# Second product of the stick-breaking scores over 128 rows, with the queries' low parts stored twice

## The chip, the cores and the metric

The kernel runs on one NeuronCore of one Trainium2 chip. The metric is device time in microseconds (us): the median of the runs of one program. The engines are named as the profile names them: PE is TensorE's matmul, PEld its weight load, DVE VectorE, ACT ScalarE, POOL GpSimd, SP the queue that issues most DMAs.

## The reference, cut to what matters

A decoder trunk of two layers over 512 tokens of width 1024, in float32. Each layer projects the normed input into three branches (latent attention, stick-breaking attention, retention), merges them by gates and adds an MLP. The change is in the second branch, whose queries, keys and values have 8 heads of 64:

```
z = einsum('bqhd,bkhd->bhqk', q[:, start:end], k[:, :end]) * scale
before = s_idx < t_idx
log_not = where(before, log_sigmoid(-z), 0.0)
between = cumsum(log_not, axis=3, reverse=True) - log_not
a = where(before, exp(log_sigmoid(z) + between), 0.0)
out = einsum('bhqk,bkhd->bqhd', a, v[:, :end])
```

`start` and `end` bound a block of 128 queries, so the blocks see 128, 256, 384 and 512 keys.

## The kernel before

**Precision.** TensorE reads float32r, which holds fewer bits than float32. Every operand of a product is therefore split into a high part (ScalarE's copy into float32r) and a low part (VectorE's difference), and a product is made of several: a dense tile of 128 columns by 512 tokens (`mm_T`, L456) is 8 times three products, high by high (L462), high by low (L463), low by high (L464), all with 128 rows of contraction and 512 columns, added up in one PSUM bank. `mm_N` (L466) does the same with 256 columns (L474 to L476). The weights stream from DRAM in chunks of up to 1 MB and are split in units (L104), up to four units at a time in the buffers `whi` and `wlo`.

**Stick-breaking operands.** Heads go in pairs. `put_q` (L909) reads a dense tile's bank with the queries of one pair, head 0 in partitions 0 to 63 and head 1 in 64 to 127, scales it to `f`, and writes three tiles: `a` with head 0's high part in both halves, `b` with head 1's high part in both halves, and `lo` with the two low parts, each in its own half. `put_k` (L924) writes for head 0 [high | low] and for head 1 [low | high]. All are tiles of a ring of 44 slots of 128 by 512 (named `slot`); a tile given back goes to the ring's end.

**The scores.** `stick_breaking`'s `first` (L585) makes one unit: pair p, query tile i, both heads. For a head the first product (L592) takes the high queries, stored twice, against [high | low] keys: 128 rows of contraction give high by high and high by low at once. The second (L593) takes the low queries, 64 rows, against the 64 rows of the high keys. Both add into one half of a two-bank PSUM tile `z`. The number of columns is 128 (i + 1), but at least 256. Then VectorE masks (L541), ScalarE takes the sigmoids, VectorE the running product (L604) and the product of both (L605). Two units later TensorE transposes the result (L548), and after a pair's fourth unit multiplies it with V (L556, in halves of 64 columns).

**Order.** The units are put between the steps of dense tiles by the driver: `advance` (L278) lets a unit through when a count of dense work has come far enough, so 16 units of a layer are spread over about 120 us of dense products. In this stage the dense products have two banks, `d`, in turn. A scheduler of the framework then orders the instructions of each engine. Pairs 0 and 1 get their queries and keys before the units start, pairs 2 and 3 while they run. Retention's scores (L691) are products of 64 rows too, on the two halves in turn; they are not touched.

Of the kernel before, what the change touches and what calls it, by code (L numbers as in the profile page):

```python
# [28 lines left out]
GATE_RUN = (2, 2, 4)  # tiles of gates before their branch products  # L29
SC = 96.0**-0.5  # L30

# columns of w_in
# [3 lines left out]
# columns of the constant pack  # L36
# [8 lines left out]
# rows of the gain pack  # L45
# [3 lines left out]
class Weights:  # L49
    """Streams weight chunks from DRAM and splits each unit into two float32r parts."""  # L50
# [16 lines left out]
    def chunk(self, srcs, k, cols, units):  # L67
        """srcs: list of (dram view [p, k, c], column); units: list of (k0, k1, c0, c1, form)"""
        c = len(self.chunks)
        self.chunks.append((srcs, k, cols))  # L70
        self.left.append(len(units))
        for u in units:
            self.units.append((c, u))
# [18 lines left out]
    def split(self):  # L92
        nc = self.nc
        u = self.n_split
        c, (k0, k1, c0, c1, form) = self.units[u]
        s = self.free.popleft()
        self.slot[u] = s
        self.n_split += 1
        src = self.raw(c)[:, k0:k1, c0:c1]
        nk, w = k1 - k0, c1 - c0  # L100
        if form is None:
            hi = self.his[s][:, : nk * w].rearrange("p (k c) -> p k c", c=w)
            lo = self.los[s][:, : nk * w].rearrange("p (k c) -> p k c", c=w)
            self.last = (nc.scalar.copy(hi, src).ins, nc.vector.tensor_sub(lo, src, hi.bitcast(F32)).ins)  # L104
        elif form == "kv":
            # [head, key | value, 64] to [key | value, head, 64]
            hi = self.his[s][:, : nk * w].rearrange("p (k c) -> p k c", c=w)
            lo = self.los[s][:, : nk * w].rearrange("p (k c) -> p k c", c=w)
            for k in range(nk):
                a = src[:, k].rearrange("p (h s d) -> p h s d", s=2, d=64)  # L110
                b = hi[:, k].rearrange("p (s h d) -> p h s d", s=2, d=64)
                nc.scalar.copy(b, a)
                nc.vector.tensor_sub(lo[:, k].rearrange("p (s h d) -> p h s d", s=2, d=64), a, b.bitcast(F32))
        else:
            # a head's 96 columns of w_uq, as [64 | 32 | 32 swapped] or [32 | 32 swapped | 64]
            w = 128
            hi = self.his[s][:, : nk * w].rearrange("p (k c) -> p k c", c=w)
            lo = self.los[s][:, : nk * w].rearrange("p (k c) -> p k c", c=w)
            if form == 0:
                parts = [(0, 0, 96), (96, 80, 16), (112, 64, 16)]  # L120
            else:
                parts = [(64, 0, 64), (0, 64, 32), (32, 80, 16), (48, 64, 16)]
            for dst, at, n in parts:
                nc.scalar.copy(hi[:, :, dst : dst + n], src[:, :, at : at + n])
            for dst, at, n in parts:
                nc.vector.tensor_sub(
                    lo[:, :, dst : dst + n], src[:, :, at : at + n], hi[:, :, dst : dst + n].bitcast(F32)
                )
        self.views = getattr(self, "views", {})
        self.views[u] = (hi, lo)  # L130
        self.left[c] -= 1
        if self.left[c] == 0:
            self.dma()
# [20 lines left out]
def trunk_kernel(  # L154
# [23 lines left out]
    # ---------------------------------------------------------------- buffers  # L178
# [36 lines left out]
    # the functions of one table set are issued together  # L215
# [11 lines left out]
    def table(out, in_, func, **kw):  # L227
        """an activation from the table set in use"""
        i = nc.scalar.activation(out, in_, func, **kw).ins
        tc.add_manual_dep(i, phase["first"].name, order, reason="table set")  # L230
        phase["all"].append(i)

    # ---------------------------------------------------------------- driver
# [24 lines left out]
    def lend():  # L258
        """between attentions their banks serve the dense products"""
        dt.extend(spare)  # L260
# [8 lines left out]
    def evacuate(ps, fn):  # L269
        """run fn a little later; then ps may be written again"""  # L270

        def go():
            fn()
            waiting[id(ps)] = False

        defer(go)
# [38 lines left out]
    # ---------------------------------------------------------------- weights  # L315
# [3 lines left out]
    def plan_T(ap, width=256):  # L319
        """columns for transposed outputs, in units of 128"""  # L320
        v = planes(ap, 0)
        nk, cols = v.shape[1], v.shape[2]
        for c in range(0, cols, width):
            w = min(width, cols - c)
            step = 1024 // nk
            W.chunk([(v[:, :, c : c + w], 0)], nk, w, [(0, nk, a, a + min(step, w - a), None) for a in range(0, w, step)])
# [53 lines left out]
    # ---------------------------------------------------------------- constants  # L380
# [30 lines left out]
    # per-token statistics -----------------------------------------------------  # L411
    def to_rstd(ms, n, width, power=-0.5):
        """(ms / n + EPS) ** -0.5 for a [128, width] sum of squares"""
        a = tiny()
        nc.vector.tensor_scalar(a[:, :width], ms, 1.0 / n, EPS, op0=ALU.mult, op1=ALU.add)
        r = tiny()
        nc.gpsimd.tensor_tensor(r[:, :width], a[:, :width], mhalf[:, :width], op=ALU.pow)
        return r

    def token_sums(parts, n=NT):  # L420
        """sums over the partitions of all parts [128, 128 n] as [128 tokens, n]"""
# [8 lines left out]
    def row_sums(ps, sq):  # L430
        """sums over the partitions of sq, on every partition"""
        nc.tensor.matmul(ps, ones.to_broadcast([P, P]), sq, start=True, stop=True)

    def spread_to(ps, r, n=NT):
        """ps[:, token] = r[token] on every partition"""
# [10 lines left out]
    def split_to(hi, lo, src, g=None):  # L446
        """hi + lo = src * g"""
# [7 lines left out]
    # products -----------------------------------------------------------------  # L455
    def mm_T(ps, wh, wl, xs):  # L456
        """ps [128 columns, 512 tokens]; wh, wl: per k [128, 128]; xs: per k (hi, lo)"""
# [9 lines left out]
    def mm_N(ps, wh, wl, xs, t):  # L467
        """ps [128 tokens, N]; wh, wl: per k [128, N]"""
# [13 lines left out]
    class Later:  # L482
        """parts that a deferred step still has to emit"""
# [12 lines left out]
    def tile_T(xs, evac):  # L496
        """the next unit of 128 columns"""
# [7 lines left out]
    def tiles_N(n_units, evac):  # L505
        """the next units, stacked along k, for every token tile"""
# [10 lines left out]
    # ---------------------------------------------------------------- attention  # L517
    flatA = aT.rearrange("p r c -> p (r c)")

    def put_A(i, e, ps):  # L520
        """store the transposed blocks j = 0..i of query tile i and parity e"""
# [16 lines left out]
    def mask(z, i, m):  # L538
        """mask the diagonal blocks of query tile i"""
# [44 lines left out]
    def stick_breaking(qT, kT, v, yb):  # L584
        def first(p, i):  # L585
# [4 lines left out]
            for e in range(2):  # L590
                r = slice(e * 64, (e + 1) * 64)
                nc.tensor.matmul(z[:, e, :M], qT[p][e][:, tok], kT[p][e][:, :M], start=True, stop=False)  # L592
                nc.tensor.matmul(z[:, e, :M], qT[p][2][r, tok], kT[p][e][r, :M], start=False, stop=True)  # L593
            mask(z, i, strict)
            # a[t] = sigmoid(z[t]) * product over t' > t of sigmoid(-z[t'])
# [58 lines left out]
    def retention(l, rq, rk, rv, rg, yc):  # L654
# [28 lines left out]
        def scores(t):  # L683
            # within the chunk, [key, query]
# [19 lines left out]
        def outputs(t):  # L704
            c = st[t]
            y = c["y"] = rot(zt)[:, 0]
            for p in range(PAIRS):
                b = slice(p * P, (p + 1) * P)
                if t:
                    # the state is zero between a pair's heads  # L710
# [9 lines left out]
            if t < NT - 1:  # L720
                # state after the chunk
# [25 lines left out]
        def norms(t):  # L747
            # group norm and gate, natural layout
# [15 lines left out]
            # 2 * silu  # L764
# [42 lines left out]
    # ---------------------------------------------------------------- set-up  # L807
    def setup():
# [35 lines left out]
        def tables():  # L844
            """cos and sin of positions * frequencies"""
# [30 lines left out]
            # per token: cos cos | -sin sin, over sqrt(96)  # L876
# [8 lines left out]
    # ---------------------------------------------------------------- a layer  # L885
    def layer(l, box):
        """box['next']: per-token rstd [128, 4] of the layer's input, once known"""
# [18 lines left out]
        # ---- stick-breaking inputs  # L906
        sq, sk, sv, yb = {}, {}, [get() for _ in range(NT)], {}

        def put_q(p):  # L909
            # per head [hi | hi], and the lo parts of the pair  # L910
            def go(ps):
                f, a, b, lo = get(), get(R), get(R), get(R)
                nc.vector.scalar_tensor_tensor(f, in0=ps, scalar=0.125, in1=rstd_b, op0=ALU.mult, op1=ALU.mult)
                for t, r in ((a, slice(0, 64)), (b, slice(64, 128))):
                    nc.scalar.copy(t[r], f[r])
                    nc.vector.tensor_sub(lo[r], f[r], t[r].bitcast(F32))
                nc.scalar.copy(a[64:128], f[0:64])
                nc.scalar.copy(b[0:64], f[64:128])
                put(f)
                sq[p] = (a, b, lo)  # L920
# [3 lines left out]
        def put_k(p):  # L924
            # per head [hi | lo] or [lo | hi]
# [68 lines left out]
        # ---- latent vectors  # L994
# [26 lines left out]
        def stat_c(key, n):  # L1021
            # the latents still lack their token's rstd, which this folds in
# [39 lines left out]
        # ---- latent attention inputs  # L1062
# [67 lines left out]
        # ---- gates and branches  # L1130
# [58 lines left out]
        # ---- retention inputs, rotated  # L1189
# [45 lines left out]
        # ---- output projection, residual  # L1235
        stats = {}

        def new_x(m, g):
            """xm[m] is final: square it, split it"""
# [26 lines left out]
        # ---- MLP  # L1266
# [92 lines left out]
    # ---------------------------------------------------------------- run  # L1359
# [10 lines left out]
def _constants():  # L1370
    """tables that depend on shapes alone"""
# [29 lines left out]
def _layout(inputs):  # L1401
    """the program's inputs, in its order: x by columns, the gains and positions by partitions"""
# [29 lines left out]
```

## Time and profile before

| What | us |
|---|---|
| median of 3 runs | 1877.92 (1877.71 to 1878.12) |
| span of the profiled execution | 1875.9 |
| PE busy in it | 1857.7 |
| PEld busy | 1533.4 |
| DVE busy | 1064.1 |
| ACT busy | 717.4 |

The span runs from the first to the last instruction of one profiled execution. Products are pipelined, so an engine that is busy for 99% of the span may still be at less than its rate: the distance between the starts of two products tells more than how long one of them is.

### The profile page before, as it was taken

How to read it: one execution, taken by the hardware profiler on the slowest of the kernel's cores; microseconds unless marked ns; L12 is line 12 of the kernel's file. 1: busy time of each engine (PE TensorE's matmuls, PEld its weight loads, DVE VectorE, ACT ScalarE, POOL GpSimd, SP SyncE). 2: the span in 40 equal slices, each digit the busy share in tenths (PEclk: the TensorE clock that was granted, in tenths of full speed). 3: DMA queues.
4: the chain of work that ended last, by engine and by line, in shares of the span. 5: the costliest groups of instructions: out<-in, count | busy, mean ns of one | idle time of the engine just before them, and what ended most of it. 6: DMA issues, size and time to landing. Idle time of an engine off the chain costs nothing.

```text
span 1875.9 us, 23563 instructions
## 1 busy us (share of the span) xinstructions
PE 1857.7 (99%) x9668; PEld 1533.4 (82%) x9668; DVE 1064.1 (57%) x1706; ACT 717.4 (38%) x1191; POOL 42.5 (2%) x57
## 2 busy tenths in 40 slices
PE   8999999999999999999999999999999999999998
PEld 7878877988888888888897787779888888888887
DVE  6775566577555444444638647646764654444456
ACT  5555444233243222323436454432333432323244
POOL 1000000001000000000000000000010000000000
PEclk9999999999999999999999999999999999999999
DMA  5220132122432322332423112221224233223324
GB/s 182 83 86 25 48 100 79 57 69 89 132 104 93 107 93 90 96 105 92 129 76 102 46 36 80 68 88 59 79 90 135 90 99 104 90 90 103 100 92 133
DMA packets 163980, 169.81 MB, mean 91 GB/s; under 512 B 5920, under 2 KB 160048, under 8 KB 163872
## 3 DMA queue, kind: packets, MB, share of 16 engines
q1 hardware_dynamic: 161360, 160.97, 27.4%
q0 software_dynamic: 2368, 7.30, 1.2%
q8 instruction: 76, 1.25, 0.3%
q14 instruction: 32, 0.26, 0.0%
q10 hardware_dynamic: 144, 0.03, 0.0%
HBM read 164.09 MB, written 4.19 MB: 90 GB/s over the span
## 4 chain that ended last, share of the span: by engine, by line
PE 98%; DMA 1%; DVE 1%; issue 0%; ACT 0%; POOLq 0%; SPq 0%; DVEq 0%
PE d L462 24%; PE d L464 24%; PE d L463 24%; PE d L474 4%; PE d L475 4%; PE d L476 4%; PE t L556 3%; PE t L548 2%; PE z L627 2%; PE z L593 1%; PE z L592 1%; DMA raw<-in_w_in_dram 1%; PE z L715 1%; PE z L476 1%; PE z L475 1%; PE z L474 1%
## 5 line engine op out<-in xcount | busy, mean ns | idle before, releaser
L104 ACT CAST whi<-raw 128x1024 fp32r<-128x1024 f32 (+1 forms) x292 | 305.9, 1049 | 672.5 <-PE d L463 552.9
L104 DVE TENSOR_TENSOR wlo<-raw,whi 128x1024 fp32r<-128x1024 f32 (+1 forms) x292 | 354.9, 1216 | 222.2 <-ACT whi L104 221.2
L462 PE MATMUL d<-xh,whi 128*128 128x512 f32 x1072 | 425.5, 397 | 7.0 <-ACT whi L104 7.0
L464 PE MATMUL d<-xh,wlo 128*128 128x512 f32 x1072 | 420.7, 393 | 0.6 <-DVE wlo L104 0.5
L463 PE MATMUL d<-xl,whi 128*128 128x512 f32 x1072 | 421.1, 393 | 0.1
L462 PE MATMUL d<-slot,whi 128*128 128x512 f32 (+1 forms) x960 | 368.5, 384 | 0.3 <-DVE slot L1309 0.3
L464 PE MATMUL d<-slot,wlo 128*128 128x512 f32 (+1 forms) x960 | 362.6, 379 | 0.0
L463 PE MATMUL d<-slot,whi 128*128 128x512 f32 (+1 forms) x960 | 362.1, 379 | 0.0
L462 PEld LDWEIGHTS d<-xh,whi 128*128 128x128 f32 x1072 | 201.9, 188 | 51.8 <-ACT whi L104 7.5
L464 PEld LDWEIGHTS d<-xh,wlo 128*128 128x128 f32 x1072 | 201.8, 188 | 44.5 <-DVE wlo L104 1.7
L463 PEld LDWEIGHTS d<-xl,whi 128*128 128x128 f32 x1072 | 202.0, 188 | 43.1 <-issue 2.4
L462 PEld LDWEIGHTS d<-slot,whi 128*128 128x128 f32 x960 | 180.3, 188 | 37.3 <-DVE slot L1309 0.5
L463 PEld LDWEIGHTS d<-slot,whi 128*128 128x128 f32 x960 | 180.3, 188 | 36.7 <-issue 0.5
L464 PEld LDWEIGHTS d<-slot,wlo 128*128 128x128 f32 x960 | 180.2, 188 | 36.9
L474 PE MATMUL d<-whi,xh 128*128 128x256 f32 x544 | 156.6, 288 | 0.0
L475 PE MATMUL d<-wlo,xh 128*128 128x256 f32 x544 | 155.1, 285 | 0.0
L476 PE MATMUL d<-whi,xl 128*128 128x256 f32 x544 | 154.9, 285 | 0.0
L1295 DVE TENSOR_TENSOR slot<-d,rkv_b 128x512 f32<-128x512 f32 x56 | 38.7, 691 | 150.0 <-PE d L464 150.0
L476 PEld LDWEIGHTS d<-whi,xl 128*128 128x128 f32 x544 | 104.1, 191 | 2.6 <-issue 2.6
L475 PEld LDWEIGHTS d<-wlo,xh 128*128 128x128 f32 x544 | 104.2, 191 | 2.4 <-issue 2.3
L474 PEld LDWEIGHTS d<-whi,xh 128*128 128x128 f32 x544 | 104.1, 191 | 1.7 <-issue 0.6
L449 ACT CAST slot<-slot 128x512 fp32r<-128x512 f32 x72 | 44.9, 624 | 88.2 <-DVE slot L1285 87.8
(204 smaller groups left out, 1865.9 us busy)
## 6 DMA issues: line engine op xcount, KB each, us to landing
raw<-in_w_in_dram SPq DMA_DIRECT2D x53, 1024.0 KB, 5.2
raw<-in_w_down_dram SPq DMA_DIRECT2D x36, 1024.0 KB, 5.1
raw<-in_w_up_dram SPq DMA_DIRECT2D x32, 1024.0 KB, 5.3
raw<-in_w_branch_dram SPq DMA_DIRECT2D x24, 512.0 KB, 3.4
raw<-in_w_out_dram SPq DMA_DIRECT2D x8, 1024.0 KB, 5.0
raw<-in_mla_w_uq_dram SPq DMA_DIRECT2D x4, 576.0 KB, 3.8
slot<-in_x_dram SPq DMA_DIRECT2D x8, 256.0 KB, 5.8
raw<-in_w_in_dram SPq DMA_DIRECT2D x4, 512.0 KB, 4.1
```

The costliest lines, as they stand in the source:

```text
L104: self.last = (nc.scalar.copy(hi, src).ins, nc.vector.tensor_sub(lo, src, hi.bitcast(F32)).ins)
L449: nc.scalar.copy(hi, src)
L462: nc.tensor.matmul(ps[:, :w], wh[k], h, start=(k == 0), stop=False)
L463: nc.tensor.matmul(ps[:, :w], wh[k], o, start=False, stop=False)
L464: nc.tensor.matmul(ps[:, :w], wl[k], h, start=False, stop=(k == n - 1))
L474: nc.tensor.matmul(ps, h, wh[k], start=(k == 0), stop=False)
L475: nc.tensor.matmul(ps, h, wl[k], start=False, stop=False)
L476: nc.tensor.matmul(ps, o, wh[k], start=False, stop=(k == n - 1))
L548: nc.tensor.transpose(ps[:, m * P : (m + 1) * P], a[:, e, j * P : (j + 1) * P], ident)
L556: nc.tensor.matmul(ps[e * 64 : (e + 1) * 64, j * P :], v[j][:, h * 64 : (h + 1) * 64], get_A(e, j), start=(j == 0), stop=(j == NT - 1), sk ...
L627: nc.tensor.matmul(z[:, e, :N], qT[h][:, i * P : (i + 1) * P], kT[h][:, :N], start=True, stop=True)
L1295: nc.vector.tensor_mul(t, ps, rstd2_b)
```

## The change

The low queries of a pair get two tiles in place of one, one for each head, with the head's low part in both halves. The second product takes all 128 rows of that tile and all 128 rows of the key tile, so it also adds low by low, which was left out before. `put_q` runs eight times (4 pairs, 2 layers). The diff also drops comments, which is left out here.

```diff
@@ stick_breaking, first
             for e in range(2):
-                r = slice(e * 64, (e + 1) * 64)
                 nc.tensor.matmul(z[:, e, :M], qT[p][e][:, tok], kT[p][e][:, :M], start=True, stop=False)
-                nc.tensor.matmul(z[:, e, :M], qT[p][2][r, tok], kT[p][e][r, :M], start=False, stop=True)
+                nc.tensor.matmul(z[:, e, :M], qT[p][2 + e][:, tok], kT[p][e][:, :M], start=False, stop=True)
@@ layer, put_q
-                f, a, b, lo = get(), get(R), get(R), get(R)
+                f, a, b, la, lb = get(), get(R), get(R), get(R), get(R)
                 nc.vector.scalar_tensor_tensor(f, in0=ps, scalar=0.125, in1=rstd_b, op0=ALU.mult, op1=ALU.mult)
-                for t, r in ((a, slice(0, 64)), (b, slice(64, 128))):
+                for t, lo, r, o in ((a, la, slice(0, 64), slice(64, 128)), (b, lb, slice(64, 128), slice(0, 64))):
                     nc.scalar.copy(t[r], f[r])
                     nc.vector.tensor_sub(lo[r], f[r], t[r].bitcast(F32))
-                nc.scalar.copy(a[64:128], f[0:64])
-                nc.scalar.copy(b[0:64], f[64:128])
+                    nc.vector.tensor_sub(lo[o], f[r], t[r].bitcast(F32))
+                    nc.scalar.copy(t[o], f[r])
                 put(f)
-                sq[p] = (a, b, lo)
+                sq[p] = (a, b, la, lb)
```

## Rows read from the trace of the kernel before

**Rows 1.** The page: busy us (share of the span) and instructions of each engine.
```profile
PE 1857.7 (99%) x9668; PEld 1533.4 (82%) x9668; DVE 1064.1 (57%) x1706; ACT 717.4 (38%) x1191; POOL 42.5 (2%) x57
```

**Rows 2.** TensorE's waits, whole span: who for whom, us, times, longest.
```profile
PE d L462 <- ACT whi L104: 7.0, 2, 6.6
PE t L425 <- ACT slot L1311: 1.3, 1, 1.3
PE t L437 <- POOL small L417: 1.1, 1, 1.1
PE d L474 <- DVE slot L1083: 1.0, 2, 0.5
...
```

**Rows 3.** The cores' spans and mean granted clock.
```profile
core 0: 1875.9 us, clock 0.998
```

**Rows 4.** Timeline of PE around a unit of 256 columns: start, us, instruction.
```profile
64.11 0.39 PE L463 MATMUL d<-xl,whi 128*128 128x512 f32 x1
64.33 0.28 PE L592 MATMUL z<-slot,slot 128*128 128x256 f32 x1
64.55 0.38 PE L593 MATMUL z<-slot,slot 64*128 64x256 f32 x1
64.86 0.38 PE L592 MATMUL z<-slot,slot 128*128 128x256 f32 x1
65.17 0.38 PE L593 MATMUL z<-slot,slot 64*128 64x256 f32 x1
65.48 0.50 PE L464 MATMUL d<-xh,wlo 128*128 128x512 f32 x1
65.81 0.39 PE L462 MATMUL d<-xh,whi 128*128 128x512 f32 x1
66.05 0.40 PE L463 MATMUL d<-xl,whi 128*128 128x512 f32 x1
```

**Rows 5.** Timeline of PE, dense products of 256 columns and a unit's first.
```profile
1073.14 0.28 PE L474 MATMUL d<-whi,xh 128*128 128x256 f32 x1
...
1073.50 0.28 PE L592 MATMUL z<-slot,slot 128*128 128x256 f32 x1
```

**Rows 6.** Timeline of PEld at the unit of rows 4, idle time in brackets.
```profile
64.11 0.19 PEld L592 LDWEIGHTS z<-slot,slot 128*128 128x128 f32 x1
64.54 0.18 PEld L593 LDWEIGHTS z<-slot,slot 64*128 64x128 f32 x1 [0.24 <-issue]
64.86 0.19 PEld L592 LDWEIGHTS z<-slot,slot 128*128 128x128 f32 x1
```

**Rows 7.** Line 593: products by shape, and idle time before its loads (us, times).
```profile
L593 PE MATMUL z<-slot,slot x64: 377/410/503, 64.5 to 1098.5; 64*128 64x256 f32 x32, 64*128 64x384 f32 x16, 64*128 64x512 f32 x16
its engine sat idle before it (us, times) until:
  issue: 11.0, 45
```

**Rows 8.** Timeline of PE, a unit of 384 columns and one of 512.
```profile
73.25 0.34 PE L592 MATMUL z<-slot,slot 128*128 128x384 f32 x1
...
74.97 0.60 PE L980 MATMUL t<-ident,slot 128*128 128x128 f32 x4
...
78.74 0.40 PE L592 MATMUL z<-slot,slot 128*128 128x512 f32 x1
...
80.70 0.39 PE L463 MATMUL d<-xl,whi 128*128 128x512 f32 x1
```

**Rows 9.** Lines 916 and 931 on DVE: ns shortest/median/longest.
```profile
L916 DVE TENSOR_TENSOR slot<-slot,slot x16: 674/687/691, 42.0 to 1005.4; 64x512 fp32r<-64x512 f32 x16
...
L931 DVE TENSOR_TENSOR slot<-slot,slot x16: 684/686/689, 46.5 to 1017.9; 64x512 fp32r<-64x512 f32 x16
```

**Rows 10.** Two stretches of 20 us: busy us and instructions by engine, clock, DMA.
```profile
80.00:100.00 20.00, 20.00 (x91) 15.11 (x90) 18.38 (x31) 11.09 (x20) 0.00 (x0) 1.00 0.18 53
...
990.00:1010.00 20.00, 20.00 (x83) 14.86 (x83) 19.41 (x36) 15.61 (x30) 0.00 (x0) 1.00 0.43 132
```

**Rows 11.** Timeline of DVE, in both layers.
```profile
76.54 0.42 DVE L605 TENSOR_TENSOR work<-work,slot 128x255 f32<-128x255 f32 x1
...
1007.42 0.68 DVE L928 TENSOR_TENSOR slot<-d,rstd_b 128x512 f32<-128x512 f32 x1
1008.01 1.22 DVE L104 TENSOR_TENSOR wlo<-raw,whi 128x1024 fp32r<-128x1024 f32 x1
...
1014.68 0.69 DVE L928 TENSOR_TENSOR slot<-d,rstd_b 128x512 f32<-128x512 f32 x1
1015.28 1.22 DVE L104 TENSOR_TENSOR wlo<-raw,whi 128x1024 fp32r<-128x1024 f32 x1
```

**Rows 12.** Timeline of PE, a transpose of stick-breaking weights.
```profile
81.86 0.27 PE L548 MATMUL t<-ident,work 128*128 128x128 f32 x1
```

**Rows 13.** Timeline of PE around retention's scores, products of 64 rows.
```profile
387.91 1.16 PE L691 MATMUL z<-aT 64*128 64x128 f32 x16
389.01 0.50 PE L462 MATMUL d<-xh,whi 128*128 128x512 f32 x1
```

## The prediction

> **What bounds the kernel now.** I read the page's busy times first, then TensorE's waits, then the stick-breaking stages of the trace product by product. TensorE is busy for 1857.7 us of a span of 1875.9 us, VectorE for 57% and ScalarE for 38% [rows 1]. In the list of TensorE's waits the whole execution has about 11 us, of which 7.0 us are for split weights [rows 2]; asked for the two stick-breaking stages alone (60 to 184 us and 980 to 1112 us) that list is empty. The granted clock is 0.998 over the span [rows 3], the 2.4 GHz level. So in these stages the time is what TensorE's own queue of products takes, and a change is worth what it does to the distance from one product's start to the next. Busy time won't tell that: the products overlap, and a 512-column product is shown as 0.39 us long though the next starts 0.23 us after it [rows 4].
>
> The reader should now look at one score unit [rows 4]. The dense products ahead of it start 0.23 us apart. Then come the unit's four products of 256 columns: 128 rows at 64.33, 64 rows at 64.55, 128 rows at 64.86, 64 rows at 65.17, and the dense product behind them at 65.48 us. The steps are 0.22, 0.31, 0.31 and 0.31 us, and the dense product behind the unit needs 0.33 us until its successor, where 0.23 is usual. In a run of dense products of the same 256 columns, all of 128 rows, three steps take 0.36 us, 0.12 us each [rows 5]. The weight loads show why: a dense product's weights are loaded while the product ahead still runs, but those of the 64-row product start at 64.54, 0.01 us before the product itself, after 0.24 us in which the loader sat idle and waited for nothing that the profile shows; those of the next 128-row product start with it, at 64.86 [rows 6]. In sum the loader stood idle 11.0 us ahead of the 64-row loads, 45 times [rows 7]. The stall is there on each way from 128 rows to 64 and on each way back.
>
> **The change, part by part.** *Removed: the 64-row products.* There are 64 of them, 32 of 256 columns, 16 of 384 and 16 of 512 [rows 7], two to a unit, so 16, 8 and 8 units of the 32 (4 pairs, 4 query tiles, 2 layers). *Put in their place:* 64 products of 128 rows with the same columns. The operand that moves is the same tile, only in its whole height; the trace has no such product on this tile, so its price lies between two rows: the stream of [rows 5], 0.12 us for 256 columns and 0.23 us for 512 [rows 4], and the step that a 128-row product of the unit has today, 0.22 to 0.31 us, which would be no gain. I take the stream: what is new is a 128-row product behind a 128-row product of the same columns, and that is what the stream's rows are; a product that adds to a bank written just before is no exception, as the dense ones do that all the time. For 384 columns I take 0.17 us, halfway, an estimate.
>
> Worked out from the start of a unit's first product to the start of the second product behind the unit:
> - 256 columns: 64.33 to 65.81 is 1.48 us [rows 4]; at stream rate four products and one dense one are 4 x 0.12 + 0.23 = 0.71. Gain 0.77 us.
> - 384 columns: 73.25 to 74.97 is 1.72 us [rows 8]; 4 x 0.17 + 0.23 = 0.91. Gain 0.81 us.
> - 512 columns: 78.74 to 80.70 is 1.96 us [rows 8]; 5 x 0.23 = 1.15. Gain 0.81 us.
>
> 16 x 0.77 + 8 x 0.81 + 8 x 0.81 = 25.3 us. Some units are not in one piece: a dense product, a transpose or the products with V stand between their halves. Each 64-row product is entered and left once all the same, so they count like the others, except where the neighbour is itself a 128*64 product with V, which keeps a switch of its own. I take 25 us.
>
> *Added: 16 subtractions on VectorE* (put_q runs 8 times and now writes each low part into both halves). The low part that is written today, 64x512, takes 687 ns, and put_k's, which also writes the other half than it reads, 686 ns [rows 9]; the new ones are of the two kinds. 16 x 0.69 = 11.0 us of VectorE's time. I cost it at nothing, and the cover has to be named, as the engine is nearly full where half of them fall: 18.38 of 20 us from 80 to 100, 19.41 of 20 from 990 to 1010 [rows 10]. There four new ones come within two dense tiles and push VectorE's later work back by up to 2.75 us. Who waits for VectorE there? First the dense banks: two take turns, and the reads of two tiles running are 7.26 us apart (L928 at 1007.42 and 1014.68 [rows 11]), so a bank read 2.75 us later is still free some 4 us before TensorE comes back to it. Then the low halves of the weights: they are split in turn with the tiles (L104 at 1008.01 and 1015.28 [rows 11]), up to four units held at once, so this split is for a tile that is not the next one. Then the unit's transposes, which wait for the last L605: the second unit of layer 0 has it at 76.96 us (76.54 + 0.42 [rows 11]) and is transposed from 81.86 [rows 12]. All that is longer than 2.75 us, and TensorE's own gain there is some 0.8 us per unit, two or three units in such a stretch. If the cover fails, it fails in these two stretches: 2 x 2.75 = 5.5 us. If every one of the 16 lay on the path it would be 11.0.
>
> *Moved or kept:* nothing is issued to another queue, and no DMA is added or moved. ScalarE's four copies per pair stay, the crosswise ones now interleaved with the halves. A pair's queries and keys hold six tiles of the ring of 44 in place of five; with four pairs (24), the four of V, the first latents and the scratch tiles I count under 40, so I take it that no tile has to be awaited.
>
> A rule of the Trainium skill speaks against the change. Rows that bear on it first: retention's 64-row products, which follow each other on alternate row halves, are 16 in 1.10 us from the first's start to the next dense product's, 0.07 us each with both switches in it [rows 13]; so 64-row products can be cheap. The Trainium skill, TensorEngine Tiling (Array Packing), sections Theoretical Speedup and When to Use Tiling, says that for a contraction of up to 64 rows two row tiles run independently, up to twice the throughput; by it the second products should stay 64 rows high and be worth half a stream step each. The measured steps of 0.31 us in [rows 4] don't agree with that for this order of products, where a 128-row one stands between any two of them.
>
> **Rivals.**
> 1. *The stall goes, but VectorE's additions reach TensorE.* For it: [rows 10]. Against it: the slack above. Gain 25 less 5.5, up to 11: 1858 to 1864 us.
> 2. *Nothing is removed*: the stall belongs to the second product of a pair on a bank, whatever its rows. Against it: dense products share a bank 24 times at stream rate, and the step back to 128 rows is as long. About 1878 us.
> 3. *Slower: the 64-row products run beside their neighbours today*, as retention's do, and at full height each costs a whole step where it cost half. Half the stream steps of 64 products are (32 x 0.12 + 16 x 0.17 + 16 x 0.23) / 2 = 5.1 us, so 1883 us. It decides if a 64-row product and its switches took less than one stream step; they take 0.31 us against 0.12 [rows 4, 5].
>
> **How the numbers follow.** The profiled execution has a span of 1875.9 us; the median of the runs is 1877.92, so 2.0 us lie outside it, and I let them stand. 1877.9 - 25 = 1853 us. Chances: the forecast 0.82, rival 1 0.12, rival 2 0.03, rival 3 0.03. The range: below, if each unit saves 0.1 us more than the clean ones show, 3 us, 1850; above, it reaches into rival 1, to the 5.5 us of the two full stretches and a little more, 1860. That leaves out under 2 in 10. A measurement of this kernel can tell about 0.2%, 3.8 us, from no change. Faster by more: the forecast and rival 1, 0.94; within it 0.03; slower 0.03.
>
> **What would show it.** In the changed profile the second product of a unit should be 128*128, its step 0.12, 0.17 and 0.23 us, its weight load 0.1 us or more ahead of it, with no idle time of the loader named "issue" before it, and the dense step behind a unit 0.23 us. L916 and its new neighbour should show 32 subtractions of about 0.69 us in place of 16, and the list of TensorE's waits should still be empty between 60 and 175 us and in layer 1's stage. The prediction is wrong if the steps stay at 0.3 us (rival 2), or if TensorE waits for L104, L913 or L605 in those stages (rival 1).

## The result, and the profile after

The changed kernel takes 1852.88 us (median of 4 runs, 1852.79 to 1853.41) where the kernel before takes 1877.82 on the same chip (4 runs, 1877.69 to 1878.12): a ratio of 0.9868, 95% interval 0.9854 to 0.9882, 24.9 us less. The span of the profiled execution went from 1875.9 to 1851.6 us. The forecast was 1853.0.

The page's busy times, which answer to [rows 1]:

```profile
PE 1833.3 (99%) x9668; PEld 1531.7 (83%) x9668; DVE 1073.0 (58%) x1722; ACT 714.7 (39%) x1191; POOL 41.8 (2%) x57
```

TensorE has the same number of products and is busy 24.4 us less; VectorE has 16 instructions more and 8.9 us more work. The timeline of PE at the first unit, to be read beside [rows 4] (after the change the unit's lines are L591 and L592):

```profile
65.29 0.39 PE L464 MATMUL d<-xh,wlo 128*128 128x512 f32 x1
65.52 0.28 PE L591 MATMUL z<-slot,slot 128*128 128x256 f32 x1
65.63 0.28 PE L592 MATMUL z<-slot,slot 128*128 128x256 f32 x1
65.75 0.28 PE L591 MATMUL z<-slot,slot 128*128 128x256 f32 x1
65.87 0.28 PE L592 MATMUL z<-slot,slot 128*128 128x256 f32 x1
65.99 0.39 PE L462 MATMUL d<-xh,whi 128*128 128x512 f32 x1
66.22 0.40 PE L463 MATMUL d<-xl,whi 128*128 128x512 f32 x1
```

The steps are 0.11, 0.12, 0.12, 0.12 and, behind the unit, 0.23 us: 0.70 from its first product to the second product behind it, where [rows 4] has 1.48. A unit of 384 columns takes 0.93 us to the second product behind it (74.25 to 75.18), where [rows 8] has 1.72. The one of 512 takes 1.25 (78.60 to 79.85) where [rows 8] has 1.96: its first product stands behind transposes and takes 0.32 us, and the steps after that are 0.23:

```profile
74.25 0.34 PE L591 MATMUL z<-slot,slot 128*128 128x384 f32 x1
...
74.95 0.39 PE L463 MATMUL d<-xl,whi 128*128 128x512 f32 x1
75.18 0.40 PE L464 MATMUL d<-xh,wlo 128*128 128x512 f32 x1
...
78.60 0.48 PE L591 MATMUL z<-slot,slot 128*128 128x512 f32 x1
78.92 0.39 PE L592 MATMUL z<-slot,slot 128*128 128x512 f32 x1
...
79.61 0.40 PE L462 MATMUL d<-xh,whi 128*128 128x512 f32 x1
79.85 0.40 PE L463 MATMUL d<-xl,whi 128*128 128x512 f32 x1
```

The weight loads at the first unit stand a whole product ahead again (those of the second product at 65.52, its product at 65.63; [rows 6] had 64.54 and 64.55):

```profile
65.30 0.19 PEld L591 LDWEIGHTS z<-slot,slot 128*128 128x128 f32 x1
65.52 0.19 PEld L592 LDWEIGHTS z<-slot,slot 128*128 128x128 f32 x1
65.64 0.19 PEld L591 LDWEIGHTS z<-slot,slot 128*128 128x128 f32 x1
```

The view of the second products' line has nothing under idle time now, where [rows 7] has 11.0 us of "issue". TensorE's waits are those of [rows 2] and 0.3 us more, so VectorE's added work has not come to the surface, though 20 us of layer 1's stage are fuller still (beside [rows 10], 19.41):

```profile
980.00:1000.00 20.00, 20.00 (x97) 16.61 (x97) 19.74 (x37) 14.25 (x26) 0.00 (x0) 1.00 0.43 131
```

The two subtractions, lines 915 and 916 of the changed kernel (beside [rows 9]), cost what was taken for them:

```profile
L915 DVE TENSOR_TENSOR slot<-slot,slot x16: 654/686/691, 43.0 to 996.6; 64x512 fp32r<-64x512 f32 x16
...
L916 DVE TENSOR_TENSOR slot<-slot,slot x16: 684/686/691, 43.7 to 997.9; 64x512 fp32r<-64x512 f32 x16
```

How near it came can be read at the dense banks. The last read of a bank with keys in layer 1 (L928 at 1014.68 in [rows 11], L927 after the change) has to be over before TensorE starts the next tile on that bank. In the kernel before it ended at 1015.37 and that tile started at 1021.36 us, 6.0 us later. In the changed kernel it ended at 1005.61 and the tile started at 1006.12, 0.5 us later:

```profile
1021.36 0.39 PE L462 MATMUL d<-xh,whi 128*128 128x512 f32 x1
```

```profile
1004.94 0.67 DVE L927 TENSOR_TENSOR slot<-d,rstd_b 128x512 f32<-128x512 f32 x1
```

```profile
1006.12 0.40 PE L462 MATMUL d<-xh,whi 128*128 128x512 f32 x1
```

### The profile page after: what moved, and what is told of

Read it like the earlier page. It is cut to its first block, busy times and chain, and to the rows that moved or that the text cites. A ratio compares the mean times of both kernels' runs of the same rounds, so it can differ in the third digit from the quotient of the medians.

```text
span 1851.6 us, 23585 instructions
## 1 busy us (share of the span) xinstructions
PE 1833.3 (99%) x9668; PEld 1531.7 (83%) x9668; DVE 1073.0 (58%) x1722; ACT 714.7 (39%) x1191; POOL 41.8 (2%) x57
## 3 DMA queue, kind: packets, MB, share of 16 engines
q8 instruction: 76, 1.25, 0.3%
## 4 chain that ended last, share of the span: by engine, by line
PE 98%; DMA 1%; DVE 1%; issue 0%; ACT 0%; POOLq 0%; SPq 0%; DVEq 0%
PE d L462 24%; PE d L464 24%; PE d L463 24%; PE d L475 4%; PE d L474 4%; PE d L476 4%; PE t L556 3%; PE t L548 2%; PE z L626 2%; DMA raw<-in_w_in_dram 1%; PE z L714 1%; PE z L476 1%; PE z L475 1%; PE z L474 1%; PE z L591 1%; PE z L592 1%
```

## The experiments

Two questions were left to settle: whether it is the change of height that costs, or the place of the 64-row product, its bank or its order; and whether VectorE's additions are free or hide a part of the gain. In the list below "before" was run on the same chip each time and gave 1877.74 to 1877.86 us.

**Both heads' 64-row products side by side.** The kernel before, in another order:

```diff
             for e in range(2):
-                r = slice(e * 64, (e + 1) * 64)
                 nc.tensor.matmul(z[:, e, :M], qT[p][e][:, tok], kT[p][e][:, :M], start=True, stop=False)
+            for e in range(2):
+                r = slice(e * 64, (e + 1) * 64)
                 nc.tensor.matmul(z[:, e, :M], qT[p][2][r, tok], kT[p][e][r, :M], start=False, stop=True)
```

> The kernel before with the four products of a unit in another order: both heads' first products, then both heads' 64-row second products side by side (on the two row halves and two banks). Theory of the switch: a unit has one way into 64 rows and one way back in place of two each. From rows of before: steps of 0.12, 0.21, 0.01 (64-row products on two halves start together, as retention's do), 0.31 and then 0.33 us for the dense product behind, 0.98 in place of 1.48 us at 256 columns; likewise 1.15 for 1.72 at 384 and 1.32 for 1.96 at 512: 16 x 0.50 + 8 x 0.57 + 8 x 0.64 = 17.7 us, so 1860 us; if the two don't run together, 4.8 us less gain, 1865. Rival, the order alone was at fault and a 64-row pair costs one step with no price for the switch: 30 us gain, 1848 us, below the changed kernel. Rival, the stall belongs to the second product on a bank whatever its rows: 1878 us.

Measured: 1862.6 us, ratio 0.9918 (0.9903 to 0.9933), 15.1 us less than before. Its timeline of PE at the first unit (L591 the first products, L594 the 64-row ones, merged in pairs):

```profile
64.22 0.39 PE L591 MATMUL z<-slot,slot 128*128 128x256 f32 x2
64.54 0.39 PE L594 MATMUL z<-slot,slot 64*128 64x256 f32 x2
64.86 0.50 PE L464 MATMUL d<-xh,wlo 128*128 128x512 f32 x1
65.19 0.40 PE L462 MATMUL d<-xh,whi 128*128 128x512 f32 x1
```

Two 64-row products take 0.39 us together, about as long as one alone in [rows 4] (0.38): they do run at the same time. But the way in and the way back are still there once per unit: 0.32 us over the pair of first products, 0.32 over the 64-row pair, and 0.33 for the dense product behind. The sum, 0.97 us, is the 0.98 that was expected, and lies between 1.48 before and 0.70 after. The total falls 2.6 us short of 17.7. In 4 of the 32 units the scheduler has put other work between the two 64-row products; by the expectation's terms that is 2.4 us (two units of 512 columns, one of 384, one of 256). One of them:

```profile
102.26 0.50 PE L594 MATMUL z<-slot,slot 64*128 64x512 f32 x1
102.69 0.49 PE L462 MATMUL d<-xh,whi 128*128 128x512 f32 x1
...
106.83 0.49 PE L594 MATMUL z<-slot,slot 64*128 64x512 f32 x1
107.25 0.50 PE L462 MATMUL d<-xh,whi 128*128 128x512 f32 x1
```

So both rivals fall: the order alone doesn't do it (1848 was asked), nor is it the second product on a bank (1878).

**One head taken back to 64 rows.** The changed kernel with

```diff
+                r = slice(0, 64) if e == 0 else slice(0, 128)
-                nc.tensor.matmul(z[:, e, :M], qT[p][2 + e][:, tok], kT[p][e][:, :M], start=False, stop=True)
+                nc.tensor.matmul(z[:, e, :M], qT[p][2 + e][r, tok], kT[p][e][r, :M], start=False, stop=True)
```

> The changed kernel with head 0's second product taken back to 64 rows, head 1's left at 128. Theory of the switch, each 64-row product pays for its own way in and back: half of the gain is lost, 1877.8 - 12.5 = 1865.3 us. Rival, a unit pays once for having any 64-row product in it: nearly all of the gain is lost, 1875 us or more.

Measured: 1865.27 us (ratio 0.9933, 0.9918 to 0.9947), where 1865.3 was expected; the runs lie 0.8 us apart, so the second decimal is luck. 32 products of 64 rows cost 1865.27 - 1852.88 = 12.4 us, 0.39 us each. In one unit the two kinds stand side by side:

```profile
64.46 0.28 PE L592 MATMUL z<-slot,slot 128*128 128x256 f32 x1
64.67 0.38 PE L593 MATMUL z<-slot,slot 64*128 64x256 f32 x1
64.98 0.39 PE L592 MATMUL z<-slot,slot 128*128 128x256 f32 x1
65.20 0.28 PE L593 MATMUL z<-slot,slot 128*128 128x256 f32 x1
65.32 0.40 PE L462 MATMUL d<-xh,whi 128*128 128x512 f32 x1
```

The 64-row product takes 0.31 us until the next start and makes the step behind it 0.22; head 1's 128-row product takes 0.12 and the dense product follows at once. The price belongs to each change of height, not to the unit.

**The order at 128 rows.** The changed kernel with the order of the first experiment.

> The changed kernel with its four products of a unit in the order of the first experiment: both first products, then both second ones, all of 128 rows. Theory of the switch: the order has no price where no product changes the height, 1852.9 us within 1 us. Rival, part of the first experiment's gain came from the order itself (the second product no longer right behind the first on its bank): below 1850 us.

Measured: 1852.64 us (ratio 0.9867, 0.9852 to 0.9881), no difference from the changed kernel. In these kernels the order had a price only where it set how often the height changes.

**The added subtractions alone.** The changed kernel's `put_q`, with the second products read from 64 rows of the new tiles:

```diff
+                r = slice(e * 64, (e + 1) * 64)
-                nc.tensor.matmul(z[:, e, :M], qT[p][2 + e][:, tok], kT[p][e][:, :M], start=False, stop=True)
+                nc.tensor.matmul(z[:, e, :M], qT[p][2 + e][r, tok], kT[p][e][r, :M], start=False, stop=True)
```

> The changed kernel's 16 added subtractions and its added tiles, with the second products kept at 64 rows (each reads its half of the new tiles). Theory of the switch, with the additions covered: as before, 1877.8 us within 1 us. Rival, VectorE's additions reach TensorE: 2.7 to 11 us longer, 1880.5 to 1889 us.

Measured: 1879.42 us, ratio 1.0007 (0.9997 to 1.0017), but over 10 runs from 1877.22 to 1881.01, a wider spread than any other here, and a median above the expected 1 us. The runs go by the mean granted clock: the two at 0.998 took 1877.22 and 1877.39 us, those at 0.997 took 1879.24 to 1879.72, those at 0.996 took 1880.88 and 1881.01. In the profiled run, which has 0.996, two stretches are at half the clock (windows: busy us of PE, PEld, DVE, ACT, POOL, then the granted clock, DMA):

```profile
132.70:136.50 3.80, 3.80 (x21) 2.49 (x19) 3.03 (x8) 2.58 (x6) 0.86 (x1) 1.00 0.79 265
136.60:139.90 3.30, 3.30 (x13) 2.77 (x13) 2.32 (x7) 2.11 (x4) 0.62 (x1) 0.50 0.00 0
140.10:141.40 1.30, 1.30 (x13) 1.20 (x11) 0.33 (x1) 0.27 (x1) 0.00 (x0) 1.00 0.00 0
1065.10:1068.30 3.20, 3.20 (x18) 3.20 (x17) 1.51 (x6) 1.52 (x3) 0.00 (x0) 0.50 0.00 0
```

Two times 3.3 us at 1.2 in place of 2.4 GHz lose about 3.3 us, and 1879.1 - 3.3 = 1875.8 is the span before, 1875.9. TensorE's list of waits has 0.5 us more than [rows 2]. So at the full clock this kernel takes as long as before, and the 1.7 us of the median are the clock's and not waits for VectorE. But they go with this kernel: 8 of its 10 runs took over 1879.2 us, none of the 13 runs of the kernel before on the same chip did (1877.32 to 1879.03), and 12 of those had 0.998. How the added subtractions or tiles bring the falls about is not shown.

The first fall on TensorE's timeline, products of one column ahead of it and dense ones of 256 columns in it:

```profile
134.10 1.05 PE L425 MATMUL t<-ones,slot 128*128 128x1 f32 x8
...
138.01 0.41 PE L476 MATMUL d<-whi,xl 128*128 128x256 f32 x1
138.23 0.41 PE L474 MATMUL d<-whi,xh 128*128 128x256 f32 x1
```

**The 128-row product without any subtraction.** The kernel before, with only the slice of rows taken off:

```diff
-                nc.tensor.matmul(z[:, e, :M], qT[p][2][r, tok], kT[p][e][r, :M], start=False, stop=True)
+                nc.tensor.matmul(z[:, e, :M], qT[p][2][:, tok], kT[p][e][:, :M], start=False, stop=True)
```

> The kernel before, its low tile as it is (head 0's low part in the upper half, head 1's in the lower), but both heads' second products take all 128 rows of it: no added subtraction, no added tile. In place of a head's low by low this adds the other head's low queries by the head's low keys, a term that the reference doesn't have. Theory of the switch, with the additions covered: as the changed kernel, 1852.9 us within 1 us. Rival, VectorE's additions cost something in the changed kernel: lower by that, 1842 to 1850 us.

Measured: 1852.87 us (ratio 0.9867, 0.9852 to 0.9882) against 1852.88 for the changed kernel. The whole gain is in the height of the product; storing the low parts twice neither adds to it nor takes from it. VectorE has 11 us less work here for the same time, but this kernel adds a term that the reference doesn't have; the change stores the low parts twice so that the added term is the head's own.

**How far VectorE's cover reaches.** The changed kernel with each added subtraction issued n times, n being 2, 4 and 8 in three kernels; four and eight were run first:

```diff
-                    nc.vector.tensor_sub(lo[o], f[r], t[r].bitcast(F32))
+                    for _ in range(n):
+                        nc.vector.tensor_sub(lo[o], f[r], t[r].bitcast(F32))
```

> The changed kernel with each added subtraction issued four times over (64 in place of 16, the same values written again): 48 x 0.69 = 33 us more of VectorE's time, of which 12 x 0.69 = 8.3 us in each of the two full stretches. Theory of the cover: the slack of 4 to 5 us behind VectorE there is passed by some 4 us in each, so 1853 to 1861 us, and TensorE's waits, if any, lie in those stretches. Rival, VectorE's work goes to the time: 1853 + 33 = 1886 us.

> The same with eight times: 112 x 0.69 = 77 us more of VectorE's time than in the changed kernel, 28 x 0.69 = 19 us in each full stretch. Theory of the cover: it is gone there, 10 to 15 us of waits in each, 1873 to 1883 us. Rival, VectorE's work goes to the time: 1930 us.

> The changed kernel with each added subtraction issued twice (32 in place of 16): 16 x 0.69 = 11 us more of VectorE's time. Four and eight times gave 1873 and 1911 us, a rise of 38 us for 44 us of work; that line meets the changed kernel's 1852.9 at some 10 us of added work, so if the cover has an edge it lies about here: 1853 to 1857 us, with no wait of TensorE over 1 us that the changed kernel lacks. Rival, there is no edge and the rise begins with the first subtraction (20 us for the 33 us of four times): 1852.9 + 11 x 20 / 33 = 1859.6 us.

| added subtractions | us | ratio to before (interval) |
|---|---|---|
| 0 (previous experiment) | 1852.87 | 0.9867 (0.9852 to 0.9882) |
| 16 (the change) | 1852.88 | 0.9868 (0.9854 to 0.9882) |
| 32 | 1865.49 | 0.9936 (0.9919 to 0.9952) |
| 64 | 1872.95 | 0.9975 (0.9965 to 0.9984) |
| 128 | 1910.9 | 1.0173 (1.0156 to 1.019) |

All three expectations missed, the theory of the cover by 8 to 28 us beyond its upper end; the rivals missed too: the price from the first subtraction on, as 16 cost nothing and 32 cost more than it said, and all of VectorE's work in the time (1886 and 1930 us). At the changed kernel's amount of work the cover holds; it ends between the change and its double. TensorE's waits of the kernel with 32:

```profile
PE d L462 <- ACT whi L104: 6.7, 1, 6.7
PE d L462 <- DVE slot L928: 2.6, 1, 2.6
PE z L591 <- ACT work L229: 2.5, 2, 1.5
...
PE z L475 <- DVE wlo L104: 1.3, 1, 1.3
...
PE t L548 <- DVE aT L531: 1.0, 2, 0.8
```

Here the wait for a dense bank, on PE and then on DVE:

```profile
1009.51 0.28 PE L592 MATMUL z<-slot,slot 128*128 128x256 f32 x1
1012.37 0.50 PE L462 MATMUL d<-xh,whi 128*128 128x512 f32 x1 [2.58 <-DVE slot L928]
```

```profile
1009.79 0.69 DVE L917 TENSOR_TENSOR slot<-slot,slot 64x512 fp32r<-64x512 f32 x1
1010.51 1.22 DVE L603 TENSOR_TENSOR_SCAN slot<-slot,ones 128x512 f32<-128x512 f32 x1
1011.65 0.67 DVE L928 TENSOR_TENSOR slot<-d,rstd_b 128x512 f32<-128x512 f32 x1
```

The read of the bank (L928) stands behind a repeated subtraction and a running product, and the clock falls right after TensorE's idle time:

```profile
1013.40:1016.70 3.30, 3.30 (x9) 2.61 (x8) 3.30 (x8) 1.36 (x4) 0.00 (x0) 0.50 0.62 174
```

The new waits in the list come to 2.6 + 2.5 + 1.3 + 1.0 and a smaller one, 8 us, and the stretch at half the clock to 1.7; of the 11.5 us between the spans (1863.1 and 1851.6) about 2 are not accounted for by these two. TensorE's products also stand in another order in this kernel than in the changed one, and what that costs was not tried apart. Not all waits lie in the two full stretches: the 1.3 us for a weight's low half come ahead of the units (between 40 and 60 us), the 2.5 us for score tiles behind those stretches, 1.0 in layer 0 and 1.5 in layer 1. The mean granted clock is 0.995 with 64 subtractions and 0.987 with 128, where the changed kernel has 0.998; of the 58 us between the spans of the last two (1909.8 and 1851.6) some 21 are the clock's, an estimate: 1909.8 x 0.013 less 1851.6 x 0.002. With 128 subtractions the list is led by waits for VectorE's copies of transposes:

```profile
PE t L548 <- DVE aT L531: 11.7, 5, 4.3
```

## Why the prediction was right

*The bound.* Right: TensorE's steps in the two stick-breaking stages gave the time; its waits changed by 0.3 us. *The stall and its owner.* Right, and shown by three runs: one head back at 64 rows loses half of the gain, two 64-row products side by side lose 0.27 us per unit of 256 columns against the change, and the rows' height alone, with no other edit, has all of it. *The price of the new product.* The stream of [rows 5] was taken for it; 0.12, 0.17 and 0.23 us are measured. *The sum.* 25.3, taken as 25; 24.9 between the medians, 24.3 between the spans. The units shown gained 0.78 us at 256 columns and 0.79 at 384, where 0.77 and 0.81 were forecast; the one of 512, behind transposes, gained 0.71 in place of 0.81.

*The rule that spoke against the change.* The Trainium skill, TensorEngine Tiling (Array Packing), section Theoretical Speedup, is borne out as far as the pair goes: two 64-row products in 0.39 us. The Trainium skill, TensorEngine Tiling (Array Packing), section Key Properties, says that changing the tiling mode, and not merely the tile, drains the engine; the first experiment agrees, with no delay between the two row halves and a way in and back around them. Followed alone, the first rule would have spoken against a change worth 24.9 us; the pairing that it suggests reaches 15.1 of them.

*The cover.* Its outcome was right, 0 us for 16 subtractions, but only just, and that is luck. The prediction left the dense bank some 4 us after a delay of 2.75, and set TensorE's own gain, 0.8 us per unit, beside it. At the last read of a bank with keys in layer 1 the margin was 6.0 us before, 2.4 with the 128-row products and no subtraction (the bank read ends at 1001.97, the next tile starts at 1004.33), and 0.5 in the changed kernel: TensorE comes back sooner, VectorE later, and the two together took 5.5 us. Twice the work, 5.5 us in place of 2.75 in each stretch, should by the prediction have cost 1 to 2 us in each, and took 12.6 in all: TensorE waits at the dense bank, at the score tiles and at the transposes too, ahead of the stretches and behind them, and once the clock fell right behind such a wait. The margin that hid the additions is smaller than one more of them each. The rivals' chance of 0.12 for a part of the gain lost there was not too high.

## What to carry to other kernels

Where TensorE is the bound, read the distance between starts and not the busy time, and look for products of another height among full ones: here each lone 64-row product cost 0.39 us more than the same product filled up to 128 rows. Filling up with copies that meet a harmless operand beat pairing the halves here, with pairs of two products of 256 to 512 columns; longer runs of 64-row products were not tried. And a cover that holds is worth a test with the doubled work: it tells whether the margin is wide or, as here, almost used.

## What the runs showed of the hardware

Two 64-row products on the two halves of the rows take together about what one takes alone (0.39 and 0.38 us at 256 columns), while the change of height costs about 0.1 us on the way in, and on the way back 0.2 at the first product and 0.1 at the one behind it. The granted clock can fall to 1.2 GHz with TensorE busy by the profile: in the run with the subtractions alone it did so at 136.6 us, after 3.8 us of lone 64-row products, products of one column and transposes, and dense products of 256 columns that had started 0.12 us apart then started 0.21 apart. The order of work alone doesn't decide it: two of the ten runs of that same program had no such fall (0.998, 1877.22 and 1877.39 us). What decides it was not tried.
